# A fourth 7-product pair in the FFN input product, and three weight pieces per double group whose low part comes from an adding DMA

## The chip, the cores and the metric

The kernel runs on one core of one Trainium2 chip. The metric is device time in microseconds (us) for one execution of the whole program, the median of several runs. Five engines work side by side on a core: TensorE (PE, the matrix product), VectorE (DVE), ScalarE (ACT), GpSimd (POOL) and SyncE (SP), each with its own queue of instructions that it takes in order. Sixteen DMA engines move data between HBM and the on-chip memory SBUF. Products leave PE through PSUM, of which the kernel uses eight banks of 128 x 512 floats.

## The reference

One layer of an encoder block on x of 256 tokens x 2048, all in float32:

```
h      = rmsnorm(x, g_mix)
q,k,v | q,k,v | gates = h @ w_in                       # 2048 x 10240
y_sb   = stick-breaking attention (8 heads)
y_ca   = chunked attention with relative bias (8 heads)
x     += (sigmoid(g_sb) * (y_sb @ w_sb_out) + sigmoid(g_ca) * (y_ca @ w_ca_out)) @ w_mix_out
g, u   = split(rmsnorm(x, g_ffn) @ w_ffn_in)           # 2048 x 11264
x     += (silu(g) * u) @ w_ffn_out                     # 5632 x 2048
x     += sigmoid(rmsnorm(x, g_ple) @ w_ple_gate) * (p @ w_ple_in)
out    = rmsnorm(x, g_final)
```

The two FFN products in the middle are what the change touches.

## The kernel before

**One product is three matmuls.** Every float32 operand is split into a high part, rounded to the matrix unit's fast float32 format, and a low part, the rounded-off rest. A product of two operands is then high x high + high x low + low x high (`three`, lines 268, 269, 270). The activations stand transposed in tables (`T1`, `T2`, `T3`: for each 128-row slice `kt`, the high and low part of 256 tokens). The weights are streamed: a *piece* is 256 rows x 512 columns, loaded from HBM by SP's queue into one of five `raw` buffers (128 x 1024 floats, 512 KB), split by `split` into `hi` (ACT, a rounding copy, line 239) and `lo` (DVE, `minus`, raw - hi, line 221), and then used by PE as the moving operand.

**Double groups.** In the FFN the work goes by *units* (double groups): two groups of 512 output columns that share the same activations. A unit's 16 slices `kt` make 8 index pairs i = 0..7 of two slices each. An index pair is 2 slices x 2 token tiles x 2 column groups, so 8 products (24 matmuls), fed by two pieces (block b = 0 and 1). For i in `PAIRS` = (2, 4, 6) it is instead done in a 7-product form of the 2 x 2 matrix product, 21 matmuls. That form needs sums of the four weight blocks (`split_pair`: four 512-wide subtractions on DVE, a 1536-wide rounding copy on ACT, a 1536-wide subtraction on DVE, and the two ordinary 1024-wide splits) and sums of the activations (`pair_sums`, `sums_of`), held in the tables `FP`, `F_more`, `F_out`. Its products go partly into the unit's own four PSUM tiles (`mm`), partly into four side tiles (`su`), which are taken from the banks of the unit before.

**The end of a unit.** When the last 7-product pair is done, `mid` (line 794 to 796) brings the four `su` tiles into a tile C of 4 x 512 on ACT and DVE; when the last piece is done, `add_sums` (L800) adds the four `mm` tiles. An input unit (`in_post`) then takes silu on ACT (L940) and two products on DVE (L942), and `hidden` puts off a task that transposes the result on PE (`tp`, L413) into the table T2. Before the first 7-product pair of the next unit takes its `su` tiles, all tasks that are waiting are run, so these transposes stand ahead of it.

**Order.** There are 11 input units (j = 0..10, 512 hidden columns each, in blocks of 3, 4 and 4; j = 0 without the 7-product form) and after each block two output units. `flush` walks through the pieces; `prefetch` loads pieces ahead while at most 5 raw buffers are taken, and splits ahead while the split pieces fit in the `hi`/`lo` buffers (three of each and a fourth). A scheduler then orders the instructions of each engine; on the chip each engine takes them in that order and waits on semaphores.

GpSimd has nearly nothing to do in the FFN. Its own DMA queue loads x again before the mix (L814) and the `pin` rows after the FFN (L980).

Of the kernel before, what the change touches and what calls it, by code (L numbers as in the profile page):

```python
# [16 lines left out]
P = 128  # L17
S = 256
# [16 lines left out]

PAIRS = (2, 4, 6)
MIX_PAIRS = (4, 6)
RAW = 5
# [3 lines left out]
def block_kernel(ctx: ExitStack, tc: tile.TileContext, x, p, w_in, w_sb_out, w_ca_out, w_mix_out,  # L42
# [79 lines left out]
    def broadcast(dst, src, pool):  # L122

        dg = pool.tile([P, S], F32, tag="dg", name="dg")
# [36 lines left out]

    def unit(wsrc, n0s, kts, lhs, forms, ext, slots, mid, post, needs, row0=0, pairs=PAIRS, alone=False, after=None):

# [8 lines left out]
        for i in range(len(kts) // 2):  # L172
# [4 lines left out]
            if i in taken:  # L177
                pieces.append(dict(pc, src=src, pair=True, first=i == taken[0], last=i == taken[-1]))
            else:
                for b in range(2):  # L180
                    pieces.append(dict(pc, src=[src[b]], block=b, first=i == 0, last=2 * i + 2 == len(kts)))

# [40 lines left out]
    def split(pc):  # L223
# [3 lines left out]
        raws = pc.pop("raw")  # L227
        state["raw"] -= len(raws)
        if pc["g"]["kind"] == "unit" and len(raws) == 2:
            return split_pair(pc, *raws)  # L230
# [11 lines left out]
        pc["lo"] = lo.rearrange("p (k n) -> p k n", n=pc["ncol"])  # L242

    def split_pair(pc, raw1, raw2):

# [3 lines left out]
        xl, xh = room[:, :1536], room[:, 1536:]  # L249
        xf = bp.tile([P, 1536], F32, tag="xf", name="xf")  # L250
        b = [raw.rearrange("p (k n) -> p k n", n=NB) for raw in (raw1, raw2)]
        t2, t3, t4 = (xf[:, NB * i : NB * i + NB] for i in range(3))
# [4 lines left out]
        nc.scalar.copy(h2, raw2)  # L257
        minus(t2, b[1][:, 1, :], b[1][:, 0, :])
        minus(t4, b[0][:, 1, :], t2)
        nc.scalar.copy(xh, xf)  # L260
# [3 lines left out]
        pc["hi"], pc["lo"] = ([t[:, NB * i : NB * i + NB] for t, n in ((u, 2), (v, 2), (w, 3)) for i in range(n)]  # L264
                              for u, v, w in ((h1, h2, xh), (l1, l2, xl)))
# [37 lines left out]
    def products(pc):  # L303
# [14 lines left out]
        else:  # L318
            group_products(pc)
        del pc["hi"], pc["lo"]  # L320

# [21 lines left out]

    state = dict(loaded=0, split=0, at=0, raw=0, hl=0, ext=0, ps=ps_mm, fourth=None)
    late = dict(ps=[ps_mm])
    started = {}

    def size(pc):
        return 0 if pc["g"]["keep"] is not None else len(pc["src"])
# [561 lines left out]
    F_out = flat[:, 6144:].rearrange("p (i c f s) -> p i c f s", i=2, c=2, f=4)  # L911
    late["F"] = [[F[:, 0], F[:, 1], F_more[:, i]] for i, F in enumerate((FP, F_out))]

# [15 lines left out]
    def hidden(dst, c, key, g):  # L929
        C = late["C"]  # L930
        later(lambda: into_table(dst, c, C[:, :2, :], key=key, pool=g["pool"],
                                 forms=lambda kt: late["F"][1][kt // 4 - 1]))

# [23 lines left out]
    for blk, nk in enumerate(FF_BLOCKS):  # L957
        key = f"h{blk}"
        for c in range(nk // 4):
            j = k0 // 4 + c  # L960
            unit(w_ffn_in[0], (j * NB, D_FF + j * NB), range(KD), T3, lambda kt: late["F"][0][kt // 4 - 1], rooms(T1),
                 C_slots, mid, (in_post if j else first_post)(T2, c, key), lambda kt: ("ffn", kt),
                 pairs=PAIRS if j else (), after=None if j else scale_next)
        last = blk == len(FF_BLOCKS) - 1
        for c in (0, 2):
            unit(w_ffn_out[0], (c * NB, (c + 1) * NB), range(nk), T2, lambda kt: late["F"][1][kt // 4 - 1],
                 rooms(T3 if last else T1), C_slots, mid, out_unit_post(c, last), lambda kt, key=key: (key, kt), row0=k0)
        k0 += nk
# [111 lines left out]
```

## Time and profile before

| | |
|---|---|
| median of 3 runs | 1468.09 us (1466.66 to 1469.55) |
| the profiled execution | 1465.74 us, span 1464.0 us |
| PE busy | 1450.6 us (99%) |
| DVE busy | 1210.1 us (83%) |
| ACT busy | 797.4 us (54%) |
| POOL busy | 23.2 us (2%) |
| DMA | 291.19 MB, 199 GB/s on average |

The span runs from the first to the last instruction of the execution that was profiled; 1.74 us lie around it. Busy time is counted by engine, overlapping instructions once. Times in a timeline row are start, duration, engine, line, operation, and in square brackets how long the engine had been idle and what ended that. The FFN runs from about 646 to 1370 us.

### The profile page before, as it was taken

How to read it: one execution, taken by the hardware profiler on the slowest of the kernel's cores; microseconds unless marked ns; L12 is line 12 of the kernel's file. 1: busy time of each engine (PE TensorE's matmuls, PEld its weight loads, DVE VectorE, ACT ScalarE, POOL GpSimd, SP SyncE). 2: the span in 40 equal slices, each digit the busy share in tenths (PEclk: the TensorE clock that was granted, in tenths of full speed). 3: DMA queues.
4: the chain of work that ended last, by engine and by line, in shares of the span. 5: the costliest groups of instructions: out<-in, count | busy, mean ns of one | idle time of the engine just before them, and what ended most of it. 6: DMA issues, size and time to landing. Idle time of an engine off the chain costs nothing.

```text
span 1464.0 us, 18640 instructions
## 1 busy us (share of the span) xinstructions
PE 1450.6 (99%) x6871; PEld 1213.5 (83%) x6871; DVE 1210.1 (83%) x1513; ACT 797.4 (54%) x949; POOL 23.2 (2%) x45
## 2 busy tenths in 40 slices
PE   9999999999999999999999999999999999999997
PEld 7888888888888888888888888888888888888886
DVE  6666666697888666888999999999999999999875
ACT  6455555557565444565555545555645555655652
POOL 0200000000000000000000000000000000000000
PEclk9999999999999999999999999999999999999999
DMA  8965555555666766666666566666566666666772
GB/s 299 296 182 173 173 173 180 180 173 173 210 193 203 243 187 186 206 195 177 190 196 192 184 214 201 210 201 205 189 201 211 192 202 195 207 197 205 234 234 93
DMA packets 164732, 291.19 MB, mean 199 GB/s; under 512 B 9024, under 2 KB 42096, under 8 KB 164384
## 3 DMA queue, kind: packets, MB, share of 16 engines
q1 hardware_dynamic: 162528, 281.32, 61.0%
q0 software_dynamic: 2112, 8.68, 1.9%
q8 instruction: 54, 0.88, 0.2%
q14 instruction: 38, 0.31, 0.1%
HBM read 284.19 MB, written 5.77 MB: 198 GB/s over the span
## 4 chain that ended last, share of the span: by engine, by line
PE 97%; issue 1%; DVE 1%; DMA 1%; ACT 0%; SPq 0%; POOL 0%; POOLq 0%; DVEq 0%
PE mm L269 24%; PE mm L268 23%; PE mm L270 23%; PE mm L335 8%; PE mm L337 4%; PE su L268 4%; PE su L269 4%; PE su L270 4%; PE tp L413 1%; DMA raw<-in_w_ple_in 1%; PE yp L634 0%; PE xps L467 0%; PE wt L725 0%; DVE T L746 0%; DVE lo L221 0%
## 5 line engine op out<-in xcount | busy, mean ns | idle before, releaser
L221 DVE TENSOR_TENSOR lo<-raw,hi 128x1024 fp32r<-128x1024 f32 (+1 forms) x517 | 625.1, 1217 | 151.3 <-ACT hi L239 149.5
L239 ACT CAST hi<-raw 128x1024 fp32r<-128x1024 f32 (+1 forms) x399 | 418.2, 1051 | 364.5 <-PE mm L270 249.8
L269 PE MATMUL mm<-lo,T 128*128 128x512 f32 x1391 | 543.1, 391 | 1.9 <-DVE lo L221 1.9
L270 PE MATMUL mm<-hi,T 128*128 128x512 f32 x1391 | 540.6, 390 | 0.0
L268 PE MATMUL mm<-hi,T 128*128 128x512 f32 x1391 | 515.9, 391 | 0.0
L269 PEld LDWEIGHTS mm<-lo,T 128*128 128x128 f32 x1391 | 261.3, 188 | 56.1 <-DVE lo L221 3.1
L270 PEld LDWEIGHTS mm<-hi,T 128*128 128x128 f32 x1391 | 261.2, 188 | 53.4
L268 PEld LDWEIGHTS mm<-hi,T 128*128 128x128 f32 x1391 | 260.9, 188 | 53.1
L335 PE MATMUL mm<-T,hi 128*128 128x512 f32 x512 | 180.1, 398 | 0.0
L337 PE MATMUL mm<-T,lo 128*128 128x256 f32 x512 | 140.6, 280 | 0.0
L257 ACT CAST hi<-raw 128x1024 fp32r<-128x1024 f32 x59 | 62.2, 1054 | 100.2 <-DVE raw L221 50.6
L335 PEld LDWEIGHTS mm<-T,hi 128*128 128x128 f32 x512 | 95.3, 188 | 21.3
L221 DVE TENSOR_TENSOR T<-xf,T 128x1536 fp32r<-128x1536 f32 x50 | 87.8, 1756 | 12.9 <-ACT T L260 12.7
L337 PEld LDWEIGHTS mm<-T,lo 128*128 128x128 f32 x512 | 96.3, 189 | 1.3
L221 DVE TENSOR_TENSOR xf<-raw 128x512 f32<-128x512 f32 x118 | 80.9, 685 | 17.0 <-DMA raw<-in_w_mix_out 6.0
L260 ACT CAST T<-xf 128x1536 fp32r<-128x1536 f32 x50 | 74.0, 1481 | 29.2 <-DVE xf L221 27.0
L254 ACT CAST hi<-raw 128x1024 fp32r<-128x1024 f32 x59 | 62.2, 1054 | 23.4 <-PE mm L270 13.9
L796 DVE TENSOR_TENSOR C<-su,C 128x512 f32<-128x512 f32 x72 | 47.8, 684 | 4.3 <-PE su L270 2.9
L800 DVE TENSOR_TENSOR C<-mm,C 128x512 f32<-128x512 f32 x72 | 47.7, 681 | 2.9 <-PE mm L270 2.9
L221 DVE TENSOR_TENSOR xf<-raw,xf 128x512 f32<-128x512 f32 x59 | 40.4, 685 | 0.6
L221 DVE TENSOR_TENSOR raw<-raw 128x512 f32<-128x512 f32 x59 | 40.3, 684 | 0.3
L268 PE MATMUL mm<-T,T 128*128 128x512 f32 (+1 forms) x82 | 30.2, 368 | 0.0
(301 smaller groups left out, 1370.9 us busy)
## 6 DMA issues: line engine op xcount, KB each, us to landing
raw<-in_w_ffn_in SPq DMA_DIRECT2D x176, 512.0 KB, 4.3
raw<-in_w_in SPq DMA_DIRECT2D x160, 512.0 KB, 3.7
raw<-in_w_ffn_out SPq DMA_DIRECT2D x88, 512.0 KB, 4.8
raw<-in_w_mix_out SPq DMA_DIRECT2D x32, 512.0 KB, 4.5
raw<-in_w_ple_gate SPq DMA_DIRECT2D x32, 512.0 KB, 5.2
raw<-in_w_sb_out SPq DMA_DIRECT2D x16, 512.0 KB, 4.5
raw<-in_w_ca_out SPq DMA_DIRECT2D x16, 512.0 KB, 4.2
x<-in_x SPq DMA_DIRECT2D x4, 512.0 KB, 9.9
```

The source lines that it names most:

```text
L221: nc.vector.tensor_tensor(out, a, b, ALU.subtract)
L239: nc.scalar.copy(hi[:, c : c + m], raw[:, c : c + m])
L254: nc.scalar.copy(h1, raw1)
L257: nc.scalar.copy(h2, raw2)
L260: nc.scalar.copy(xh, xf)
L268: nc.tensor.matmul(ps, xh, hi, start=a, stop=False)
L269: nc.tensor.matmul(ps, xh, lo, start=False, stop=False)
L270: state["mm"] = nc.tensor.matmul(ps, xl, hi, start=False, stop=z)
L335: nc.tensor.matmul(ps, hi[:, i, f], lhs[:, kt, :, :].rearrange("p c s -> p (c s)"), start=a, stop=False)
L337: nc.tensor.matmul(ps[:, :S], lo[:, i, f], lhs[:, kt, 0, :], start=False, stop=z)
L796: nc.vector.tensor_tensor(C[i], q, C[j], ALU.add)
L800: nc.vector.tensor_tensor(g["C"][i], g["ps"][i], g["C"][i], ALU.add)
```

## The change

For the input units the 7-product form is used at i = 1, 2, 4 and 6 (`IN_PAIRS`); the output units keep (2, 4, 6). The sums of activations for the fourth pair have a table of their own, `F4`.

In every unit from j = 1 on, the pieces (i, b) = (0, 0), (3, 0) and (5, 1) are `added` pieces (two of them in the output units of the first block). For such a piece `split_early` makes the low part without DVE: ACT rounds raw into `dhi` and writes the negative of the same rounding into `dlo` (one more ACT instruction, scale -1), and a DMA from GpSimd's queue loads the same weights once more from HBM and adds them onto `dlo`, which leaves raw - hi. There are two `dhi` and two `dlo` buffers; at most two added pieces are under way. They don't count against the `hi`/`lo` buffers.

To make room, `split_pair` keeps only one 512-wide sum in `xf` and forms the others in place in the raw buffers (the 1536-wide copy and subtraction become one of 512 and one of 1024 each), tile C has one buffer instead of two, and the small tile of `broadcast` shares another's place.

```diff
+IN_PAIRS = (1, 2, 4, 6)
+ADDED = ((0, 0), (3, 0), (5, 1))
...
+    def split_early(pc):
+
+        pool = late["pool"]
+        raw, = pc["raw"]
+        hi, lo = (pool.tile([P, 1024], F32R, tag=tag, name=tag, bufs=2) for tag in ("dhi", "dlo"))
+        nc.scalar.copy(hi, raw)
+        nc.scalar.activation(lo, raw, AF.Identity, scale=-1.0)
+        pc["hi"], pc["lo"] = (t.rearrange("p (k n) -> p k n", n=NB) for t in (hi, lo))
+        dma_x.dma_start(pc["lo"], pc["src"][0], accum_op=ALU.add)
...
     def split_pair(pc, raw1, raw2):
...
-        minus(t3, b[1][:, 1, :], b[1][:, 0, :])
-        minus(b[1][:, 0, :], b[1][:, 0, :], b[0][:, 0, :])
+        minus(t3, b22, b12)
+        minus(b12, b12, b11)
+        minus(l1, raw1, h1.bitcast(F32))
         nc.scalar.copy(h2, raw2)
-        minus(t2, b[1][:, 1, :], b[1][:, 0, :])
-        minus(t4, b[0][:, 1, :], t2)
-        nc.scalar.copy(xh, xf)
-        minus(l1, raw1, h1.bitcast(F32))
+        minus(b11, b22, b12)
+        minus(b21, b21, b11)
+        nc.scalar.copy(xh[:, 1024:], t3)
+        nc.scalar.copy(xh[:, :1024], raw1)
         minus(l2, raw2, h2.bitcast(F32))
-        minus(xl, xf, xh.bitcast(F32))
+        minus(xl[:, 1024:], t3, xh.bitcast(F32)[:, 1024:])
+        minus(xl[:, :1024], raw1, xh.bitcast(F32)[:, :1024])
...
     def prefetch():
         while state["loaded"] < len(pieces) and state["raw"] + len(pieces[state["loaded"]]["src"]) <= RAW:
             load(pieces[state["loaded"]])
             state["loaded"] += 1
+        for pc in pieces[state["split"] : state["loaded"]]:
+            if pc.get("added") and "hi" not in pc and state["adding"] < 2:
+                split_early(pc)
+                state["adding"] += 1
...
-        C = late["pool"].tile([P, 4, NB], F32, tag="C", name="C", bufs=2)
+        C = late["pool"].tile([P, 4, NB], F32, tag="C", name="C")
...
-            if kts[0] // 2 in PAIRS:
-                pair_sums(late["T3"], kts[0], late["F"][0][PAIRS.index(kts[0] // 2)])
+            if kts[0] // 2 in IN_PAIRS:
+                pair_sums(late["T3"], kts[0], late["F"][0][kts[0] // 2])
...
+    F4 = lp.tile([P, 2, 4, P], F32R, tag="F4", name="F4")
...
-                 pairs=PAIRS if j else (), after=None if j else scale_next)
+                 pairs=IN_PAIRS if j else (), after=None if j else scale_next, added=ADDED if j else ())
...
-                 rooms(T3 if last else T1), C_slots, mid, out_unit_post(c, last), lambda kt, key=key: (key, kt), row0=k0)
+                 rooms(T3 if last else T1), C_slots, mid, out_unit_post(c, last), lambda kt, key=key: (key, kt), row0=k0,
+                 added=ADDED if nk == 16 else ADDED[:2])
...
-    pin_t = lp.tile([P, 2, NT, NB], F32, tag="C", name="pi", bufs=2)
+    pin_t = lp.tile([P, 2, NT, NB], F32, tag="C", name="pi")
```

Three places show what this does to the order of instructions. The first is DVE at the end of unit j = 1. Before, the rows up to the second product with `r_ffn` (L942), after which C may be transposed:

```order
L800 TENSOR_TENSOR C<-mm_6102,C 128x512
L796 TENSOR_TENSOR C<-su_6200,C 128x512 x2
L221 TENSOR_TENSOR xf<-raw 128x512
L800 TENSOR_TENSOR C<-mm_6103,C 128x512
L221 TENSOR_TENSOR lo<-raw,hi 128x1024
L800 TENSOR_TENSOR C<-mm_6116,C 128x512
L221 TENSOR_TENSOR raw<-raw 128x512
L800 TENSOR_TENSOR C<-mm_6117,C 128x512
L221 TENSOR_TENSOR lo<-raw,hi 128x1024
L942 SCALAR_TENSOR_TENSOR C<-C,r_ffn 128x512
L221 TENSOR_TENSOR xf<-raw 128x512
L942 SCALAR_TENSOR_TENSOR C<-C,r_ffn 128x512
```

Of the change, the last twelve rows up to the same instruction (now L964; `minus` is now line 223, `T_71` is the scratch room for the sums of weights):

```order
L223 TENSOR_TENSOR T_71<-raw,T_71 128x1024
L223 TENSOR_TENSOR T_71<-xf,T_71 128x512
L223 TENSOR_TENSOR raw<-raw 128x512
L821 TENSOR_TENSOR C<-mm_6154,C 128x512
L821 TENSOR_TENSOR C<-mm_6168,C 128x512
L821 TENSOR_TENSOR C<-mm_6167,C 128x512
L223 TENSOR_TENSOR raw<-raw 128x512
L223 TENSOR_TENSOR lo<-raw,hi 128x1024
L964 SCALAR_TENSOR_TENSOR C<-C,r_ffn 128x512
L223 TENSOR_TENSOR xf<-raw 128x512
L964 SCALAR_TENSOR_TENSOR C<-C,r_ffn 128x512
L223 TENSOR_TENSOR T_71<-raw,T_71 128x1024
```

More of the next unit's weight work now stands between the additions to C: from the row `C<-su_6214` to the second product there are 21 DVE instructions (17 of 512, 4 of 1024 elements), of which 11 are weight work; before, from the row `C<-mm_6102` above, 13 instructions (11 of 512, 2 of 1024), of which 5 are.

The second place is PE at the same end of unit j = 1, where the transposes of C stand (L434, before L413). Before:

```order
L269 MATMUL mm_6453<-lo,T_5065 128x512
L270 MATMUL mm_6453<-hi,T_5065 128x512
L413 MATMUL tp<-ident,C 128x128 x2
L268 MATMUL mm_6452<-hi,T_5065 128x512
L269 MATMUL mm_6452<-lo,T_5065 128x512
L270 MATMUL mm_6452<-hi,T_5065 128x512
L268 MATMUL mm_6453<-hi,T_5065 128x512
L413 MATMUL tp<-ident,C 128x128 x6
```

Of the change:

```order
L284 MATMUL mm_6504<-dlo,T_5083 128x512
L285 MATMUL mm_6504<-dhi,T_5083 128x512
L283 MATMUL mm_6518<-hi,FP 128x512
L283 MATMUL mm_6505<-T_71,T_5083 128x512
L284 MATMUL mm_6518<-lo,FP 128x512
L285 MATMUL mm_6518<-hi,FP 128x512
L434 MATMUL tp<-ident,C 128x128 x8
L283 MATMUL su_6572<-hi,T_5083 128x512
```

The eight transposes now stand together, directly ahead of the first `su` product of the next unit, 54 places after the last matmul into `su_6214`; nine places ahead of them stands the first use of the `dlo` of the added piece (3, 0).

The third place is ACT ahead of that added piece. Of the change:

```order
L271 CAST hi<-raw 128x1024
L243 CAST hi<-raw 128x1024
L253 CAST dhi<-raw 128x1024
L254 ACTIVATE dlo<-raw 128x1024
L243 CAST hi<-raw 128x1024
```

The added piece has two ACT instructions where a plain piece has one, and behind the second its DMA on GpSimd's queue (`dlo<-in_w_ffn_in`, L256) begins.

More of the change, by code (lines that the diff above doesn't have):

```diff
@@ L160, in group, with unit @@
             ))
-    def unit(wsrc, n0s, kts, lhs, forms, ext, slots, mid, post, needs, row0=0, pairs=PAIRS, alone=False, after=None):
+    def unit(wsrc, n0s, kts, lhs, forms, ext, slots, mid, post, needs, row0=0, pairs=PAIRS, alone=False, after=None, added=()):
         if not alone:
@@ L180, in unit @@
                 for b in range(2):
-                    pieces.append(dict(pc, src=[src[b]], block=b, first=i == 0, last=2 * i + 2 == len(kts)))
+                    pieces.append(dict(pc, src=[src[b]], block=b, first=i == 0, last=2 * i + 2 == len(kts), added=(i, b) in added))
     def load_x(c):
@@ L319, in products @@
             group_products(pc)
+        if pc.get("added"):
+            state["adding"] -= 1
         del pc["hi"], pc["lo"]
@@ L342, in group_products @@
             g["ps"] = None
-    state = dict(loaded=0, split=0, at=0, raw=0, hl=0, ext=0, ps=ps_mm, fourth=None)
+    state = dict(loaded=0, split=0, at=0, raw=0, hl=0, ext=0, ps=ps_mm, fourth=None, adding=0)
     late = dict(ps=[ps_mm])
@@ L348, in size @@
     def size(pc):
-        return 0 if pc["g"]["keep"] is not None else len(pc["src"])
+        return 0 if pc["g"]["keep"] is not None or pc.get("added") else len(pc["src"])
     def prefetch():
```

19 lines of the change are left out of this document (10 added, 9 removed).

## The prediction

> **What bounds the kernel now.** I read the page first, then the windows of single units, then what PE waited for.
>
> ```profile
> span 1464.0 us, 18640 instructions
> PE 1450.6 (99%) x6871; PEld 1213.5 (83%) x6871; DVE 1210.1 (83%) x1513; ACT 797.4 (54%) x949; POOL 23.2 (2%) x45
> DVE  6666666697888666888999999999999999999875
> ...
> PEclk9999999999999999999999999999999999999999
> ...
> PE 97%; issue 1%; DVE 1%; DMA 1%; ACT 0%; SPq 0%; POOL 0%; POOLq 0%; DVEq 0%
> ...
> PE mm L269 <- DVE lo L221: 1.9, 1, 1.9
> PE warm L506 <- POOL mhalf L97: 1.2, 1, 1.2
> PE mm L268 <- ACT hi L239: 1.2, 1, 1.2
> ...
> 953.00:995.30 42.30, 42.30 (x190) 34.91 (x189) 39.88 (x49) 24.16 (x26) 0.00 (x0) 1.00 0.61 192
> 995.30:1037.50 42.20, 42.20 (x193) 34.93 (x191) 38.92 (x48) 24.07 (x26) 0.00 (x0) 1.00 0.59 191
> ```
>
> PE is 97% of the chain of waits, and waits three times in all, never in the FFN: each matmul less is time won, as long as PE goes on never waiting. But DVE is the second bound: in the slices of the FFN it stands at 9 tenths, and in the two windows, each one input unit long (length, PE, PEld, DVE, ACT, POOL busy), it works 39 to 40 us of 42.2. What the change does to DVE decides.
>
> **The gain on PE.** Ten input units do one more index pair in 21 instead of 24 matmuls: 30 matmuls less. The chain in order of time shows what one costs there:
>
> ```profile
> 1010.96 0.68 PE mm L268 x3
> ```
>
> 0.68 / 3 = 0.227 us (the 0.39 of a single row overlaps the next), so 30 x 0.227 = 6.8 us. Transposes stay as many.
>
> **What DVE is asked for.** Its prices, and ACT's, come from rows that follow each other without a gap; what counts is the distance of starts:
>
> ```profile
> 1001.08 1.06 ACT L257 CAST hi<-raw 128x1024 fp32r<-128x1024 f32 x1 [1.92 <-issue]
> 1002.04 0.61 ACT L401 CAST T<-fm 128x512 fp32r<-128x512 f32 x1
> 1002.26 0.68 DVE L221 TENSOR_TENSOR xf<-raw 128x512 f32<-128x512 f32 x1
> 1002.86 1.22 DVE L221 TENSOR_TENSOR lo<-raw,hi 128x1024 fp32r<-128x1024 f32 x1
> 1004.00 0.68 DVE L221 TENSOR_TENSOR T<-fm,T 128x512 fp32r<-128x512 f32 x1
> ...
> 1006.83 1.76 DVE L221 TENSOR_TENSOR T<-xf,T 128x1536 fp32r<-128x1536 f32 x1 [0.41 <-ACT T L260]
> ```
>
> DVE: 0.60 for 512 elements, 1.14 for 1024, and 1.67 for 1536 (1.76 less the same overlap); ACT 0.96 for 1024. A 7-product pair costs DVE 4 x 0.60 + 2 x 1.14 + 1.67 = 6.35 us before and 6.42 after (the 1536 cut in two); a plain piece 1.14. An input unit had 3 pairs and 10 plain pieces, 30.5 us; it gets 4 pairs and 8 plain pieces, 3 of them without DVE: 31.4. So DVE gains 0.9 us of work per input unit while PE loses 0.68: about 40.4 of 41.5 us. On the average that fits; what counts is where it is bunched. Output units lose 3.2 us of DVE work (2.1 in the first block), where PE waits for nothing: no gain.
>
> **Where it is bunched.** The next unit's first pair now stands at i = 1 instead of 2, so its sums, and the transposes of C that must precede its su tiles, come sooner after the unit's end. At the end of unit j = 1 the order has 17 DVE instructions of 512 and 4 of 1024 from the first wait for the last su tile to C being ready: 17 x 0.60 + 4 x 1.14 = 14.8 us. PE has 54 places from that su matmul to the transposes: 54 x 0.227 = 12.2 us. DVE starts about 0.5 later (0.39 for the matmul and a hand-over, an estimate). So C is late by 14.8 + 0.5 - 12.2 = 3.0 us, and PE stands. The same count at the other ends of an input unit with another behind it:
>
> - j = 3: 54 places, 14.8 us of DVE: 3.0 late
> - j = 5: 57 places, 13.0 us: 0.6 late
> - j = 8: 57 places, 14.1 us: 1.7 late
> - j = 9: 49 places, 13.0 us: 2.4 late
> - j = 4 and 7: 2.0 and 0.2 in time; in front of output units (j = 2, 6, 10) over 4 in time
>
> Sum of the five: 10.8 us. How good is such a count? On the order before it gives C in time by 4.7, 5.1 and 3.5 us at j = 1, 2 and 3. The trace:
>
> ```profile
> 756.09 0.74 DVE L942 SCALAR_TENSOR_TENSOR C<-C,r_ffn 128x512 f32<-128x512 f32 x1
> 761.52 0.38 PE L413 MATMUL tp<-ident,C 128*128 128x128 f32 x2
> ...
> 798.18 0.74 DVE L942 SCALAR_TENSOR_TENSOR C<-C,r_ffn 128x512 f32<-128x512 f32 x1
> 802.82 0.38 PE L413 MATMUL tp<-ident,C 128*128 128x128 f32 x2
> ...
> 907.51 1.41 DVE L942 SCALAR_TENSOR_TENSOR C<-C,r_ffn 128x512 f32<-128x512 f32 x2
> 911.22 1.03 PE L413 MATMUL tp<-ident,C 128*128 128x128 f32 x8
> ```
>
> From the end of L942 to the transposes: 4.7, 3.9 and 2.3 us. The count is too kind by 0, 1.2 and 1.2, 0.8 on average. With that, five stalls grow by 0.8 (4.0) and j = 7 becomes 0.6 late: 10.8 + 4.0 + 0.6 = 15.4 us. I take this value, 10.8 as its lower end.
>
> **The adding DMA.** 46 pieces are loaded a second time and added. The trace has no adding DMA; the nearest are plain 512 KB loads of the same shape from GpSimd's queue (pin rows, x four at once) and from SP's (weights in the FFN):
>
> ```profile
> L980 POOL DMA_DIRECT2D pi<-pin_d x4: 722/736/749, 1331.6 to 1415.0; - x4
> DMA to landing us min/median/max: 5.1/5.5/8.6
> ...
> L814 POOL DMA_DIRECT2D x<-in_x x4: 704/717/726, 482.0 to 484.1; - x4
> DMA to landing us min/median/max: 6.3/7.9/9.5
> ...
> DMA to landing us min/median/max: 3.4/4.4/9.2
> ```
>
> Below stands 4.4 (a weight load), above 9.5 (the last of four). Adding must also read its target, so I take 7, between 5.5 and 8.6 (an estimate). Time in hand: for (3, 0) of unit j = 2, ACT's last wait for PE lies 37 matmuls ahead of dlo's first use, 8.4 us; three ACT instructions and the hand-over take 0.96 x 2 + 1.06 + 0.3 = 3.3, which leaves 5.1. Of 46 pieces, the three shortest have 4.7, 5.1 and 5.6 ((3, 0) of j = 4, 2, 6), four more 6.8 to 7.6, all others 8.8 or over. At 7 us three are late by 2.3, 1.9 and 1.4, but these stand nine places ahead of transposes that are late anyway (3.8, 3.8, 1.4 with the correction): the stalls overlap, and only 0.2 (6.8) is new. [...]
>
> **What costs nothing.** ACT gets about 4.6 us per input unit (3 x 0.96 for the negatives, some 1.5 for the pair): 29 of 41.5, in PE's shadow; without it, 4.6 us per unit. GpSimd's issues, 0.73 each, find it idle. SP issues as many loads as before; 24 MB more at 190 GB/s raise the DMA share from 0.6 to about 0.7. With one C buffer the pin loads wait for the last output unit:
>
> ```profile
> 1363.30 0.58 POOL L976 DMA_DIRECT2D gf<-in_g_final  x1 [30.20 <-PE su L270]
> 1394.64 0.75 POOL L980 DMA_DIRECT2D pi<-pin_d  x1 [16.46 <-DVE sgr L993]
> ```
>
> The first use of these rows ends at 1394; loads begun some ten us after 1363 land by 1382. If not, only the first gating waits, not PE.
>
> **Sum.** -6.8 + 15.4 + 0.2 = +8.8 us. The profiled execution took 1465.74 (span 1464.0, 1.74 around it): 1474.5. The median of the runs is 2.35 higher: 1468.09 + 8.8 = 1476.9.
>
> **The rivals.**
>
> 1. DVE's bunching is absorbed and the 6.8 us arrive: 1461.3. For: the average load fits, and before every C was ready 2 us early. Against: the order is fixed and the count errs to the other side. It needs chains some 3 us shorter at two places. 0.12.
> 2. The stalls just eat the gain: only j = 1 and 3 are late, 6.0 us: -0.8, 1467.3. It needs the correction to be wrong and the three smaller places to come in time. 0.17.
> 3. The adding DMA decides, from about 8 us to landing. At 9 the seven short pieces and three at 8.8 are late; with what overlaps counted once (3.8, 4.3, 3.4, 2.5, 3.2 at the ends, 6.5 elsewhere) that is 23.7 us: +16.9, 1485; at 9.5 about 1490. For: it shares engines with weight loads, and x reached 9.5. Against: they are single, not four at once. 0.17.
> 4. The clock: a stalled PE is given a slower clock afterwards.
>
> ```profile
> 1450.00:1464.00 14.00, 5.02 (x42) 4.82 (x41) 4.79 (x16) 1.20 (x2) 0.67 (x1) 0.82 0.36 125
> ```
>
> Idle for 9 of 14 us, PE was granted 0.82. If two stalls of 3.8 were each followed by 14 us at 0.82, 5.0 us come on top: 1482. Against: at the start, idle for 1.2 us at a time, the slices of PEclk show no lower clock. [...] 0.04.
>
> **How the numbers follow.** Forecast 0.50, rivals 0.12, 0.17, 0.17, 0.04. A measurement of this kernel tells about 0.2% (2.9 us) from no change. Faster 0.12 (rival 1), same 0.17 (rival 2), slower 0.71. The forecast's own range is 1472 (10.8 us of stalls) to 1481 (20). The range 1464 to 1488 leaves out rival 1 and rival 3's upper half.
>
> **What would show it.** Right: 30 fewer matmuls on PE; PE waiting in the FFN for DVE (C at L964, sums and lo at L223) some 10 to 20 us in all, at j = 1, 3, 5, 8, 9, 3 to 4 us at the longest; transposes starting as the second L964 ends; waits of PE for dlo of few us; adding DMAs landing in 5 to 8.6 us. Wrong: no wait of PE for DVE at these ends, or dlo waits larger than DVE's, or a granted clock below 1 in the FFN.

## The result and the profile after

The changed kernel takes 1569.07 us (median of 4 runs, 1568.47 to 1573.85), the kernel before, run beside it, 1468.82 (4 runs). The ratio is 1.0692, 95% interval 1.0667 to 1.0717: 100 us slower. Forecast were 1476.9 and a range up to 1488. The direction was right, the size was off by a factor of more than ten. The execution that was profiled is the slowest of the four, 1573.85 us.

The page of the profile after, its span and busy times, and its DMA queues (packets, MB, share of the sixteen engines' time):

```profile
span 1571.8 us, 18732 instructions
PE 1487.1 (95%) x6841; PEld 1219.2 (78%) x6841; DVE 1207.3 (77%) x1592; ACT 858.0 (55%) x1075; POOL 79.3 (5%) x91
...
q1 hardware_dynamic: 162528, 281.32, 56.9%
q0 software_dynamic: 14624, 32.80, 10.5%
```

PE issues 30 matmuls less, as forecast, and DVE works 2.8 us less. Yet PE is idle for 1571.8 - 1487.1 = 84.7 us (13.4 before), and its busy time is 36.5 us longer although it has 6.8 us less to do: the mean granted clock fell from 0.998 to 0.982, and since a matmul's row lasts 0.39 us while starts lie 0.227 us apart, gaps of up to 0.16 us count as busy. PE and DVE are further from their limits than before, ACT is as busy as it was (55% against 54%): the engines wait for each other and for DMAs. What PE waits for (line, releaser: us in total, times, longest):

```profile
PE mm L284 <- DMA dlo<-in_w_ffn_in: 39.9, 17, 5.5
PE mm L284 <- DMA dlo<-in_w_ffn_out: 12.3, 8, 3.8
PE mm L284 <- DVE lo L223: 5.6, 8, 1.9
PE mm L283 <- DVE C L817: 5.0, 8, 1.2
PE mm L284 <- DVE T L223: 3.2, 2, 1.8
PE tp L434 <- DVE C L964: 1.8, 2, 1.2
```

The first uses of 25 of the 46 added pieces stand waiting for their adding DMA, 52.2 us in all. The transposes, at which the prediction put its 15.4 us, wait 1.8. What ACT and DVE wait for after, of that what concerns raw loads:

```profile
ACT dhi L253 <- DMA raw<-in_w_ffn_in: 40.1, 20, 6.5
...
ACT dhi L253 <- DMA raw<-in_w_ffn_out: 27.2, 13, 3.7
...
DVE xf L223 <- DMA raw<-in_w_ffn_out: 32.6, 14, 4.7
...
DVE xf L223 <- DMA raw<-in_w_ffn_in: 26.0, 21, 3.5
```

Before, the same waits were few:

```profile
ACT hi L239 <- DMA raw<-in_w_ffn_out: 5.5, 2, 3.6
...
DVE xf L221 <- DMA raw<-in_w_ffn_out: 6.0, 7, 1.8
DVE xf L221 <- DMA raw<-in_w_ffn_in: 2.9, 4, 1.1
```

Weights that used to lie ready now arrive late. Of what SP's queue waits for before it may load, two rows that before were small or not there:

```profile
SPq L207 <- DVE T L223: 136.1, 59, 7.4
SPq L207 <- ACT dlo L254: 81.3, 44, 3.2
```

The first is the last subtraction of the in-place sums (before, 4.2 us for the same tile), the second the negative of an added piece. One stall in the timeline of the change, at the end of unit j = 1, shows how (start, duration, engine; in brackets the idle time and what ended it):

```profile
762.19 1.06 ACT L271 CAST hi<-raw 128x1024 fp32r<-128x1024 f32 x1 [1.62 <-PE mm L285]
...
763.15 1.04 ACT L253 CAST dhi<-raw 128x1024 fp32r<-128x1024 f32 x1
...
764.10 1.05 ACT L254 ACTIVATE dlo<-raw 128x1024 fp32r<-128x1024 f32 x1
...
765.18 8.69 SPq L207 DMA_DIRECT2D raw<-in_w_ffn_in  x4
...
765.45 1.19 POOL L256 DMA_DIRECT2D dlo<-in_w_ffn_in  x1 [13.88 <-PE mm L284]
...
769.92 0.39 PE L285 MATMUL mm<-T,T 128*128 128x512 f32 x1
...
773.54 0.50 PE L284 MATMUL mm<-dlo,T 128*128 128x512 f32 x1 [3.23 <-DMA dlo<-in_w_ffn_in]
```

ACT is released by PE, casts three times, and the adding DMA is issued at 765.45, 0.30 after the third ends. PE needs `dlo` 0.227 us after the start of its last matmul, at 770.15: 4.7 us in hand, close to the 5.1 that the prediction counted. The DMA lands 8.0 us after its issue, and PE stands 3.2 us. The same instruction of ACT, which ends at 765.15, lets SP's queue go, since it holds the raw buffer too (`SPq L207 <- ACT dlo L254: 3.2, 1, 3.2` in this window). So raw loads start beside the adding DMA, at 765.18, 765.83 and 768.77; the fourth of that row starts at 773.50. The windows around the stall (length, PE, PEld, DVE, ACT, POOL, clock, DMA share, GB/s):

```profile
762.00:764.00 2.00, 2.00 (x10) 1.68 (x9) 2.00 (x5) 1.81 (x2) 0.00 (x0) 1.00 0.00 0
764.00:766.00 2.00, 2.00 (x10) 1.66 (x9) 2.00 (x4) 2.00 (x4) 0.55 (x1) 1.00 0.00 0
...
770.00:774.00 4.00, 0.77 (x4) 0.42 (x3) 4.00 (x6) 2.66 (x3) 0.00 (x0) 1.00 1.08 268
774.00:778.00 4.00, 4.00 (x18) 3.30 (x16) 3.23 (x5) 0.52 (x1) 0.00 (x0) 0.62 0.46 136
778.00:782.00 4.00, 4.00 (x19) 3.38 (x18) 3.90 (x8) 3.76 (x7) 0.00 (x0) 0.96 0.48 131
```

For 4 us the DMA engines move nothing, and for 3.2 of them SP waits for a raw buffer; during the stall they are busy to the full, with the adding DMA among the loads. And after the stall the granted clock is 0.62 for the next 4 us. In this trace all eight stalls of 3.2 us or more are followed by 4 us at 0.50 to 0.67; of the shorter ones three are (1.8, 1.9 and 1.9 us; 0.59, 0.64 and, ahead of the FFN, 0.63), while one of 1.8 and one of 2.8 us are followed by 1.00. So the length of the stall alone doesn't decide; what else does, the trace doesn't show.

### The profile page after: what moved, and what is told of

It is laid out like the page before. It is cut to its first block, busy times and chain, and to the rows that moved or that the text cites. A ratio compares the mean times of both kernels' runs of the same rounds, so it can differ in the third digit from the quotient of the medians.

```text
span 1571.8 us, 18732 instructions
## 1 busy us (share of the span) xinstructions
PE 1487.1 (95%) x6841; PEld 1219.2 (78%) x6841; DVE 1207.3 (77%) x1592; ACT 858.0 (55%) x1075; POOL 79.3 (5%) x91
## 3 DMA queue, kind: packets, MB, share of 16 engines
q1 hardware_dynamic: 162528, 281.32, 56.9%
q0 software_dynamic: 14624, 32.80, 10.5%
## 4 chain that ended last, share of the span: by engine, by line
PE 57%; issue 17%; DMA 15%; DVE 8%; ACT 3%; POOL 1%; POOLq 0%; DVEq 0%; SPq 0%; ACTq 0%
PE mm L284 13%; PE mm L285 12%; PE mm L283 12%; PE mm L352 8%; DMA raw<-in_w_ffn_out 5%; PE mm L354 4%; DMA dlo<-in_w_ffn_in 3%; DMA raw<-in_w_ffn_in 3%; DVE lo L223 3%; DMA dlo<-in_w_ffn_out 2%; PE su L283 2%; PE su L284 2%; PE su L285 2%; DVE raw L223 1%; DVE T L223 1%
## 5 line engine op out<-in xcount | busy, mean ns | idle before, releaser
L223 DVE TENSOR_TENSOR lo<-raw,hi 128x1024 fp32r<-128x1024 f32 (+1 forms) x471 | 570.3, 1220 | 199.9 <-ACT hi L243 176.3
L243 ACT CAST hi<-raw 128x1024 fp32r<-128x1024 f32 (+1 forms) x333 | 348.5, 1049 | 319.8 <-PE mm L285 176.0
L284 PE MATMUL mm<-lo,T 128*128 128x512 f32 x1137 | 446.6, 393 | 5.6 <-DVE lo L223 5.6
L285 PE MATMUL mm<-hi,T 128*128 128x512 f32 x1137 | 442.9, 392 | 0.0
L283 PE MATMUL mm<-hi,T 128*128 128x512 f32 x1137 | 434.2, 395 | 5.3 <-DVE C L817 2.9
L283 PEld LDWEIGHTS mm<-hi,T 128*128 128x128 f32 x1137 | 214.4, 189 | 55.1 <-DVE C L817 5.4
L285 PEld LDWEIGHTS mm<-hi,T 128*128 128x128 f32 x1137 | 214.6, 189 | 44.2
L223 DVE TENSOR_TENSOR raw<-raw 128x512 f32<-128x512 f32 x207 | 141.0, 686 | 1.0
L284 PE MATMUL mm<-dlo,T 128*128 128x512 f32 x184 | 79.4, 432 | 52.3 <-DMA dlo<-in_w_ffn_in 39.9
L223 DVE TENSOR_TENSOR T<-raw,T 128x1024 fp32r<-128x1024 f32 x68 | 83.1, 1221 | 33.6 <-ACT T L275 29.6
L223 DVE TENSOR_TENSOR xf<-raw 128x512 f32<-128x512 f32 x69 | 47.7, 691 | 65.1 <-DMA raw<-in_w_ffn_out 32.6
L253 ACT CAST dhi<-raw 128x1024 fp32r<-128x1024 f32 x46 | 48.4, 1051 | 67.7 <-DMA raw<-in_w_ffn_in 40.1
L275 ACT CAST T<-raw 128x1024 fp32r<-128x1024 f32 x60 | 62.7, 1046 | 31.0 <-DVE raw L223 30.3
```

The source lines that it names most:

```text
L223: nc.vector.tensor_tensor(out, a, b, ALU.subtract)
L243: nc.scalar.copy(hi[:, c : c + m], raw[:, c : c + m])
L253: nc.scalar.copy(hi, raw)
L275: nc.scalar.copy(xh[:, :1024], raw1)
L283: nc.tensor.matmul(ps, xh, hi, start=a, stop=False)
L284: nc.tensor.matmul(ps, xh, lo, start=False, stop=False)
```

## The experiments

All numbers are medians with the ratio to the kernel before, run beside them on the same chip (1466.4, 1467.1, 1469.1, 1468.5 and 1467.8 us). Where runs are compared that did not stand beside each other, it is by what each takes over its own kernel before.

### First: the DMA, the early casts, the pair

The theory to begin with was that the adding DMA's landing makes the loss (rival 3 of the prediction, larger). The rival was that ACT's early casts and the in-place sums do. First the DMA alone is left out, then it is replaced by a plain load, with the order of PE, DVE and ACT as in the change:

```diff
-        dma_x.dma_start(pc["lo"], pc["src"][0], accum_op=ALU.add)      # e1_no_dma: line left out
+        dma_x.dma_start(pc["lo"], pc["src"][0])                        # e2_plain_dma
```

> The changed kernel without the adding DMA itself: dhi and dlo are still made by ACT, but nothing is added to dlo, so the low parts of three pieces per unit are wrong (that addition and its second load are left out). If the second load and its landing make the loss: 1465 to 1478 us, PE idle in the FFN under 15 us, all of it from DVE at the ends of input units (the order of this kernel has C late by 2.0, 1.1, 2.1, 0.4 and 0.5 us at five of them). If ACT's casts that wait for the raw load (67 us of waiting in the changed kernel) make the loss by themselves: 1520 us or more, with those waits still there. If DVE's bunching made most of the 100 us: 1540 us or more.

Measured: 1513.16 us, 1.0314 (1.0299 to 1.0329), 46.7 us over the kernel before: none of the three cases.

> The changed kernel with a plain load into dlo in place of the adding one: same bytes from HBM, same queue, same order of instructions on PE, ACT and DVE, only the addition is left out (dlo holds the weights, the result is wrong). If the adding as such is dear: landing falls from 9.0 to about 5.5 us, GpSimd's issue from 1.20 to 0.73 us, PE's waits for dlo from 52 to under 10 us, and the time to 1475 to 1500 us. If it is the second load's traffic, whatever it does: landing 8 to 9 us and 1550 us or more.

Measured: 1525.23 us, 1.0389 (1.0358 to 1.0421). Issue, landing and waits come out nearly as in the first case, the time lies between the two. What PE waits for and how the second load lands, with the plain load:

```profile
PE mm L284 <- DMA dlo<-in_w_ffn_out: 6.0, 3, 4.3
PE mm L284 <- DMA dlo<-in_w_ffn_in: 4.2, 7, 1.3
...
L256 POOL DMA_DIRECT2D dlo<-in_w_ffn_in x30: 716/716/749, 703.2 to 1314.4; - x30
...
DMA to landing us min/median/max: 4.5/6.3/9.9
```

And with the adding one, in the change:

```profile
L256 POOL DMA_DIRECT2D dlo<-in_w_ffn_in x30: 1194/1203/1245, 701.9 to 1351.2; - x30
...
DMA to landing us min/median/max: 6.6/9.0/11.9
```

The second load itself costs 12 us, the adding 41 to 44 more: it lands 2.7 us later in the median, it takes GpSimd 0.49 us longer to issue, and PE's waits for `dlo` grow from 10.2 to 52.2 us. But 47 us of the loss stand without any second load, so the theory holds for less than half. Next, one half of the change without the other:

```diff
-IN_PAIRS = (1, 2, 4, 6)
+IN_PAIRS = (2, 4, 6)              # e3_added_only
-ADDED = ((0, 0), (3, 0), (5, 1))
+ADDED = ()                        # e4_pair_only
```

> The changed kernel with three pairs (2, 4, 6) in the input units as before, the three added pieces kept. DVE has some 3 us less to do per unit than before, and no place in this order leaves it less than 3 us. If the adding DMA makes the loss: PE waits for dlo as in the changed kernel, 40 to 60 us, and the slow clock with it: 1540 to 1580 us. If the bunching by the fourth pair makes it: 1465 to 1472 us, no measurable change from before.

Measured: 1553.97 us, 1.0594 (1.0567 to 1.0621), 87.5 us over. The time is that of the first case, its reason is not: PE waits for `dlo` 13.5 us, not 40 to 60, while ACT's `dhi` casts wait 175.1 us for raw loads.

> The changed kernel with the fourth pair and no added pieces: all low parts by DVE. DVE then has about 44 us of work in an input unit of 41.5, and this order has C late by 5.6 to 5.9 us at the ends of five input units and later elsewhere. If DVE is the bound here: PE waits for DVE about 3 to 5 us in each of ten input units, 30 to 50 us, no wait for dlo: 1490 to 1515 us, and more if the clock falls after the stalls. If DVE's lateness costs nothing: 1461 us.

Measured: 1542.49 us, 1.0512 (1.0495 to 1.053), 76.1 us over, above the range of the first case, which allowed for more if the clock falls (it is 0.985). Each half alone makes most of the loss, so neither half is its cause by itself; they share something. Both keep the in-place sums, and the single tile C.

### Second: the in-place sums, the early casts and the fourth pair, each alone

The kernel before gets the new `split_pair` and nothing else:

```diff
-        xf = bp.tile([P, 1536], F32, tag="xf", name="xf")
+        t3 = bp.tile([P, NB], F32, tag="xf", name="xf")
...
-        minus(t2, b[1][:, 1, :], b[1][:, 0, :])
-        minus(t4, b[0][:, 1, :], t2)
-        nc.scalar.copy(xh, xf)
+        minus(b11, b22, b12)
+        minus(b21, b21, b11)
+        nc.scalar.copy(xh[:, 1024:], t3)
+        nc.scalar.copy(xh[:, :1024], raw1)
...
-        minus(xl, xf, xh.bitcast(F32))
+        minus(xl[:, 1024:], t3, xh.bitcast(F32)[:, 1024:])
+        minus(xl[:, :1024], raw1, xh.bitcast(F32)[:, :1024])
```

> The kernel before with one part of the change: the new split_pair, whose sums are formed in place in the raw buffers, so that the first raw buffer of a pair is held until the pair's last subtraction. Three pairs, no added pieces, two C buffers. Theory R (the raw buffers are held longer, the next loads start later, and ACT and DVE wait for weights): 1500 to 1535 us, with waits of ACT and DVE for raw loads far above the 12 us of before. Theory D (the adding DMA and the fourth pair make the loss): 1466 to 1472 us, as before.

Measured: 1515.06 us, 1.0326 (1.0309 to 1.0343): 48 us for a step that the prediction priced at 0.07 us per pair. In its trace PE waits for DVE, ACT's casts wait for raw loads, and SP waits for the sums before it may load:

```profile
PE mm L269 <- DVE C L797: 24.0, 9, 4.1
...
PE mm L270 <- DVE lo L221: 3.7, 3, 1.9
...
ACT hi L239 <- DMA raw<-in_w_ffn_in: 54.7, 25, 4.0
...
ACT hi L239 <- DMA raw<-in_w_ffn_out: 51.5, 16, 6.3
...
SPq L205 <- DVE T L221: 89.0, 49, 6.4
SPq L205 <- DVE raw L221: 82.3, 23, 6.2
```

ACT's waits for output loads were 5.5 us before. With three sums in `xf`, as before, the raw buffers are free when the sums are formed and the two ordinary splits are made. Now two of these lie in `raw1` instead, which is read until the last subtraction (`T<-raw`), behind ACT's rounding of those sums, and SP, which loads in order, waits for it. Then the fourth pair with the old split, and the added pieces with the old split; both keep the change's single tile C:

```diff
-        t3 = bp.tile([P, NB], F32, tag="xf", name="xf")
+        xf = bp.tile([P, 1536], F32, tag="xf", name="xf")
...                                  # the rest of split_pair as before
                                     # in e4_pair_only: e7_pair_old_split
                                     # in e3_added_only: e8_added_old_split
```

> The changed kernel with the fourth pair, no added pieces, and the old split_pair (sums in a buffer of 1536 elements of their own). DVE has about 43.5 us of work per input unit of 41.5. Theory R: far below the 1542 us of the same kernel with the new split_pair, 1475 to 1500 us, what is left being DVE's overload in ten input units (2 to 4 us each, less 6.8). Theory D', that DVE's work by the fourth pair made the 76 us: 1530 us or more, since this kernel gives DVE only 0.07 us less per pair.

Measured: 1513.30 us, 1.0320 (1.0305 to 1.0336), 46.2 us over: between the ranges of the two theories.

> The changed kernel with three pairs in the input units, the three added pieces, and the old split_pair. Theory R: far below the 1554 us of the same kernel with the new split_pair; 1468 to 1490 us, with some PE waits for dlo left. Theory D (the adding DMA, landing after 9 us, makes the loss): 1535 us or more.

Measured: 1514.74 us, 1.0326 (1.0307 to 1.0345), again between the two ranges. The waits for `dlo` and of ACT in the kernel with the added pieces and the old split:

```profile
PE mm L283 <- DMA dlo<-in_w_ffn_out: 3.0, 3, 1.8
PE mm L283 <- DMA dlo<-in_w_ffn_in: 1.9, 2, 1.0
...
ACT dhi L253 <- DMA raw<-in_w_ffn_in: 127.7, 29, 8.2
ACT dhi L253 <- DMA raw<-in_w_ffn_out: 74.1, 16, 7.8
```

Three steps, each taken first, cost 48, 46 and 48 us, in all 142, and the whole change 100. PE waits for `dlo` only 4.9 us in the last of them, though the DMA lands nearly as late as in the change (median 8.5 us against 9.0): here the early start does its work. What is large there is ACT's wait: 45 of the 46 early casts stand on ACT for a load that is still under way, 202 us in all, and everything behind them on ACT's queue stands too.

A rival that no run takes alone is the single tile C, which stands in every kernel here with the fourth pair or added pieces, but for the one with GpSimd's subtraction below. No wait in the change's trace is put down to it: the first instructions that write C (L815, L817) wait 5.1 us for `su` matmuls, and none for the transposes that read C before. What it costs by the order of instructions stays unknown.

### Third: is it the time in the raw buffers?

A unit takes 16 pieces in 42.2 us, one in 2.64. Five buffers allow a piece to stay 13.2 us from its load's issue to its last reader, of which landing alone takes 4.4 (before). If there is no slack in that, a sixth buffer must give the in-place sums back what they cost, and a fourth buffer less must cost the kernel before as much:

```diff
-RAW = 5
+RAW = 6          # in e5_inplace_only: e9_inplace_raw6
+RAW = 4          # in the kernel before: e10_raw4
```

> The first of these kernels (before with the new split_pair) with six raw buffers instead of five; the sixth takes the room that the smaller sum buffer leaves. Theory R: at least half of what the new split_pair costs is won back. If the in-place sums cost by their order on DVE and ACT (the wide copy waits for the last sum) and not by the buffers: no more than a quarter is.

Measured: 1485.54 us, 1.0129 (1.0114 to 1.0144): 29.5 of the 48 us are back. The waits of ACT's `hi` casts (L239) for FFN loads fall from 106.2 to 28.4 us, those of DVE's `xf` sums grow from 13.6 to 39.0.

> The kernel before with four raw buffers instead of five, nothing else. A unit of 42.2 us takes 16 loads, one per 2.64 us, so with five buffers one may be taken 13.2 us on average, with four 10.6. Theory R (the buffers' time is what bounds all these kernels, and before has little to spare): 1500 us or more, with ACT and DVE waiting for raw loads and PE for them. If the buffers have slack in the kernel before: 1466 to 1475 us.

Measured: 1512.87 us, 1.0294 (1.0279 to 1.0309), 44 us for one buffer less, with the same picture in ACT's waits:

```profile
ACT hi L239 <- DMA raw<-in_w_ffn_in: 76.9, 33, 5.8
...
ACT hi L239 <- DMA raw<-in_w_ffn_out: 66.0, 23, 7.0
```

So the kernel before had no whole buffer to spare, though PE never waited in its FFN. The sixth buffer of the run above takes the room that the narrower `xf` leaves; the kernel before with six was not run.

For the early casts the test is to let them stand later: the early split is begun one step of `prefetch` later, and on ACT it goes behind the last cast for nearer pieces. Of the edit, the lines that order ACT:

```diff
...
+        with tc.issue_after(state["cast"].ins):      # the last cast issued for a nearer piece
             split_early(pc)                          # e11: in e8_added_old_split; e12: in the change
...
```

> The kernel with three pairs, the old split_pair and the added pieces (1515 us, ACT's dhi casts waiting 202 us for the raw loads in 45 of 46 cases), with the early split put one step later: it is issued after the splits of the nearer pieces, and on ACT behind the last of their casts. Theory Q (ACT stands at a cast whose load is still under way, and the casts behind it, needed sooner, come late): dhi's waits for raw fall below 80 us and the time to 1475 to 1495 us. Theory D (it is the landing of the adding DMA): 1515 us or more, since dlo begins later, and PE's waits for dlo grow from 5 to 20 us or more.

Measured: 1504.18 us, 1.0241 (1.0225 to 1.0257), 35.1 us over the kernel before instead of 47.6; ACT's waits of `dhi` for raw loads fall from 202 to 111 us. That is Theory Q's direction, but short of both its figures; PE's waits for `dlo`, 8.7 us, stay below Theory D's.

> The changed kernel with the early split one step later, as in the run beside it. In-place sums and fourth pair stay, so Theory Q expects part of the 100 us back: 1535 to 1555 us, with fewer waits of ACT for raw loads. Theory D: 1569 us or more, with PE's waits for dlo above the 52 us of the changed kernel.

Measured: 1580.84 us, 1.0758 (1.0732 to 1.0784): 12 us slower than the change, with 65.2 us of waits for `dlo`, as Theory D has it. In the whole change the adding DMA cannot begin later without PE waiting longer for it.

Another way to relieve DVE, without early casts: GpSimd forms the low part of four plain pieces in each input unit.

```diff
+BY_POOL = ((0, 0), (3, 0), (5, 0), (7, 0))
...
-            minus(lo[:, c : c + m], raw[:, c : c + m], hi.bitcast(F32)[:, c : c + m])
+            by = nc.gpsimd if pc.get("added") else nc.vector
+            by.tensor_tensor(lo[:, c : c + m], raw[:, c : c + m], hi.bitcast(F32)[:, c : c + m], ALU.subtract)
```

> The kernel before with the fourth pair and the old split_pair, and in each input unit from the second on four plain pieces whose low part GpSimd subtracts, in its ordinary place, in place of DVE: no second load, no early cast, two C buffers. DVE has 43.5 - 4.6 = 39 us of work per unit, as much as before. If a unit's DVE work and the time of raw buffers are what counts, and GpSimd's subtraction of 1024 takes under 4 us: 1461 to 1470 us. If GpSimd's subtraction is slower than that, or slows DVE beside it: 1490 us or more.

Measured: 1547.15 us, 1.0528 (1.0512 to 1.0544), 32 us further above its kernel before than the pair with DVE doing all (78.1 against 46.2, the latter with a single tile C). The low parts in its trace (min, median and max ns; most of DVE's plain pieces have a line of their own, L243):

```profile
L223 DVE TENSOR_TENSOR lo<-raw,hi x138: 1209/1218/3434, 369.9 to 1436.5; 128x1024 fp32r<-128x1024 f32 x138
L243 POOL TENSOR_TENSOR lo<-raw,hi x40: 2392/2844/9611, 704.2 to 1349.6; 128x1024 fp32r<-128x1024 f32 x40
```

A subtraction of 1.22 us on DVE takes up to 3.43 in this kernel; the longest in the kernel before takes 1.23, and so does the longest in the change, where GpSimd subtracts no low parts. Between 700 and 1350 us DVE's means are up too: 0.85 us for the `xf` sums from raw (0.69 before), 1.94 for the 1536-wide subtraction (1.76). GpSimd's subtractions beside them are the likely cause; how the two get into each other's way no run shows.

### Fourth: one cause or several?

A sixth buffer for the fourth pair, and for the whole change; the latter needs room, so it has one added piece under way at a time, and a run with five buffers as its base.

```diff
-RAW = 5
+RAW = 6                                              # in e4_pair_only: e13_pair_raw6
...
-        hi, lo = (pool.tile([P, 1024], F32R, tag=tag, name=tag, bufs=2) for tag in ("dhi", "dlo"))
+        hi, lo = (pool.tile([P, 1024], F32R, tag=tag, name=tag, bufs=1) for tag in ("dhi", "dlo"))
...
-            if pc.get("added") and "hi" not in pc and state["adding"] < 2:
+            if pc.get("added") and "hi" not in pc and state["adding"] < 1:    # both in the change: e15_after_one
...
-RAW = 5
+RAW = 6                                              # in e15_after_one: e16_one_raw6
```

> The kernel with four pairs and the in-place sums, without added pieces (1542.5 us with five raw buffers), with a sixth raw buffer. The sixth buffer won back 29.5 us of the 48 that the in-place sums alone cost. Theory A (the time in raw buffers is what the fourth pair loses too: it takes two buffers of five at once): the sixth buffer wins at least as much again, 1500 to 1515, ACT's casts wait for raw loads under 25 us instead of 56.6 and SP's waits behind the last sums fall. Theory B (DVE's load of about 43.5 us per unit of 41.5 decides): no buffer helps, 1525 or more, with PE still waiting 25 us or more for DVE's lo and C. The loads alone put a floor under A: ten units of 43.5 instead of 42.2 us, 13 us over the kernel before, about 1480.

Measured: 1516.14 us, 1.0325 (1.0308 to 1.0343): 28 us won, close to the sixth buffer's 30 with the sums alone, and just outside Theory A's range; ACT's `hi` waits 11.1 us for FFN input loads. So the sixth buffer gives back what it gave back to the sums. The fourth pair on top of them costs as much as before: 28 us with five buffers (76.1 against 48.0) and 29 with six (47.7 against 18.4).

> The whole change, but with one added piece under way at a time (one dhi and one dlo buffer): the early split of the next added piece begins only after the last use of the one before. It is the base for the next run, which needs the room. If early casts that block ACT's queue set the loss, fewer are early and the time falls, 1530 to 1560; if the landing of the adding DMA sets it, it begins later and the time rises above 1571, with waits of PE for dlo above the 62 us of the change.

Measured: 1585.37 us, 1.0800 (1.0773 to 1.0827). (The waits for `dlo` in the change are 52.2 us, not the 62 of the expectation; here they are 76.1, as the second case has it. ACT's `dhi` casts wait 0.3 us for raw loads instead of 67.3, so `dlo` is late without these waits too.)

> The run before with a sixth raw buffer. Theory A (raw buffers are what the change runs short of): at least 25 us below the run before, and ACT's waits for raw loads (dhi, hi, xf) fall by half. Theory B (the adding DMA and its landing decide): within 10 us of the run before, waits of PE for dlo unchanged. Under A with B beside it: 25 to 35 us less, and what remains over the kernel before stands in the waits of PE for dlo.

Measured: 1578.54 us, 1.0757 (1.0727 to 1.0786): as in Theory B, with the adding DMA a sixth buffer wins 7 us, not 30. The last run keeps its order and lets the second load replace instead of add:

```diff
-        dma_x.dma_start(pc["lo"], pc["src"][0], accum_op=ALU.add)
+        dma_x.dma_start(pc["lo"], pc["src"][0])              # in e16: e17_plain_one_raw6
```

> The run with six raw buffers and one added piece at a time (1578.5 us), but the second load replaces dlo instead of adding to it, so the addition is left out of what is computed; order of PE, DVE and ACT the same. If adding alone sets the change's loss once there are enough raw buffers, PE's waits for dlo (74 us) nearly vanish and the time falls to 1490 to 1510, by more than the 44 us that the same edit won with five buffers, since the two losses then no longer cover each other. If the late start of the second load is what counts, whatever it does at its target, waits for dlo stay above 30 us and the time stays above 1530.

Measured: 1512.97 us, 1.0310 (1.0292 to 1.0327), 65 us less, just above the first range. PE's waits for `dlo`, first with adding and six buffers:

```profile
PE mm L284 <- DMA dlo<-in_w_ffn_in: 59.1, 24, 5.2
PE mm L284 <- DMA dlo<-in_w_ffn_out: 14.9, 7, 3.9
```

and with the plain load:

```profile
PE mm L284 <- DMA dlo<-in_w_ffn_in: 22.2, 10, 4.5
...
PE mm L284 <- DMA dlo<-in_w_ffn_out: 3.3, 1, 3.3
```

So there are at least two causes, and each covers part of the other: the adding DMA (41 to 44 us with five buffers, 65 with six), and weights that stay too long in the raw buffers or behind early casts (47 us without any second load). In kernels without added pieces a sixth buffer gives back 28 to 30 us; the kernel without the second load was not given one.

### The account

The runs form a ladder; each line is the time over the kernel before that ran beside it.

| step | over before | step's cost |
|---|---|---|
| in-place sums (e5) | +48.0 | +48.0 |
| fourth pair and early casts, no second load (e1) | +46.7 | -1.2 |
| second load, plain (e2) | +58.8 | +12.1 |
| adding (the change) | +100.3 | +41.5 |

The split depends on the order of the steps: taken first, the fourth pair costs 46 us, and the early casts with the adding DMA 48. From e1 on the kernels have the single tile C. What the ladder doesn't tell is how much each stall costs beyond itself. Of the 43 us (36.5 + 6.8) by which PE's busy time is too long, some 24 are the clock (1.6% of 1487, an estimate from the two mean clocks).

## Why the prediction was wrong, point by point

- **The bound and the gain on PE** were right: 6871 - 30 = 6841 matmuls. With PE waiting everywhere, the 6.8 us are not to be seen in the end.
- **"SP issues as many loads as before"** under "What costs nothing" is the step that failed first. The count is right (SP's queue moves 281.32 MB before and after), but what counts is when a buffer comes free. The text of the change said that the sums are formed in place in the raw buffers; the prediction costed that at 6.42 us of DVE instead of 6.35 and did not ask who waits for the buffers. This step alone measured +48 us, of which a sixth buffer gives back 29.5. What SP's queue waited for in the kernel before:

```profile
SPq L205 <- DVE lo L221: 913.5, 400, 7.1
SPq L205 <- DVE xf L221: 104.5, 50, 5.6
```

  Loads were issued as a buffer came free, 450 times after a wait for DVE. The row shows that DVE's reads pace the loads, not how much there is to spare: with four buffers the first of them is 888.0 us. What told it was the run with one buffer less, 44 us slower.
- **"ACT gets about 4.6 us per input unit, in PE's shadow"** took ACT's work for its cost. ACT's load rose about as counted (858.0 - 797.4 = 61 us in all), but an early cast in an in-order queue waits for its load in front of casts that are due: 67 us of such waits in the change, 202 with the old split, where casting later won 12.5 us.
- **The bunching on DVE, 15.4 us.** (The five places add up to 10.7 us, not 10.8, which changes nothing.) PE's waits for DVE in the rows above sum to 15.6 us, but not where they were forecast: the transposes wait 1.8 us, the rest lies in the `mm` products, and the kernel without the fourth pair (e5) waits more for DVE, 27.7 us. The agreement is chance. The count assumed that DVE always has its operands, but its `xf` sums wait 58.6 us for raw loads in the change; whether that is why no bunch formed, no run shows. Without relief for DVE the fourth pair costs 46 us (e7), three times the term, and there too the transposes wait only 1.8 us.
- **The adding DMA, 0.2 us**, was mis-sized. The mechanism was rival 3's, and the time in hand was nearly right where ACT is released by PE (4.7 us measured, 5.1 counted). The landing is 9.0 us in the median and up to 11.9, not 7; rival 3 put 9 us at 23.7 us of stalls in ten pieces, measured are 52.2 in 25. The time in hand was also counted too long for many pieces: from the issue of the DMA to the first use 23 pieces have less than 8.8 us, where the count had seven. The count began at ACT's last wait for PE and took the raw data as landed, but a late raw load does not pick out the pieces that stall: ahead of 18 of the 25 ACT had waited for it, and ahead of 15 of the other 21. Why the time in hand was shorter stays open. The bounds were 4.4 and 9.5 us from plain loads; adding has its median near the upper one and its longest beyond it, and 7 was an estimate between them that no row gave. Nor does a row show that the adding DMA reads its target: GpSimd's queue has the same 14624 packets and 32.80 MB with the plain load.
- **Rival 4, the clock**, was given 0.04, and acts: 0.62 in the 4 us after the stall shown. It adds to stalls that others make and is no case of its own; it belonged on every case with stalls like those eight of 3.2 us or more.
- **The range** held only cases in which one thing goes wrong and the rest of the machine keeps its slack. Three did (the in-place sums, the early casts, the adding DMA), in a kernel whose slack in buffers had not been measured.

Of the signs of being wrong under "What would show it", two came true: waits for `dlo` larger than DVE's, and a clock below 1 in the FFN.

What stays open: the 48 us of the fourth pair with in-place sums and six buffers (in its trace PE waits 34 us, most for ACT's and DVE's splits, and the clock is 0.990), and 18 of the in-place sums with six. DVE's load is a suspect for the former: with five buffers, taking three low parts per unit from DVE and putting nothing in their place (e4 against e1) wins 29 us, in spite of the early casts. But that also changes when raw buffers come free, so no run separates DVE's load, and none the single tile C. None of the sixteen kernels beats the one before.

## What to carry to other kernels

Before an edit that lets work read a streaming buffer longer, compute the time a buffer may be held (buffers times the interval between loads, 13.2 us here, of which landing takes 4.4) and ask which reader frees it last; an engine at 99% with no waits says nothing about slack, and one buffer less is a cheap way to measure it (44 us here). A prefetch put on an in-order engine is only early if its data is there: else it delays what is due behind it (with the old split 45 of 46 early casts waited on ACT, 202 us in all, and casting later won 12.5 us). Price a DMA that computes by its own measurement, not by plain loads (here 9.0 us to landing in the median against 6.3).

## What the hardware showed that was not expected

- An adding DMA keeps the sixteen DMA engines busy nearly twice as long as a plain one of the same 512 KB. GpSimd's queue takes 10.5% of 1571.8 us in the change; less the 27.8 us that it took before (1.9% of 1464.0), that is 137 us for 46 loads, 2.98 us each. With the plain load it is 6.7% of 1526.4, so 74.5 us and 1.62 each, as for SP's loads (61.0% of 1464.0 for 281.32 MB, 1.66 for 512 KB). Its row with the plain load:

```profile
q0 software_dynamic: 14624, 32.80, 6.7%
```

- One raw buffer of five is worth 44 us in a kernel whose PE never waits in the FFN.
- After each of eight stalls of 3.2 us or more in the change the granted clock is 0.50 to 0.67 for 4 us; by the mean clocks this makes some 24 us of the loss (an estimate, from 0.998 and 0.982 over 1487 us).
